# Queries and keys loaded in pieces of 64 partitions, and the stage behind v put in order by estimated engine times

## The chip, the cores and the metric

The kernel runs on one core of a Trainium2 chip. The metric is the device time of one execution in microseconds. TensorE (PE) multiplies, VectorE (DVE), ScalarE (ACT) and GpSimd (POOL) do the elementwise work, and SyncE (SP) issues nearly all transfers between DRAM and the on-chip memory; 16 DMA engines carry them.

## The reference

One encoder layer on `x` of 1024 tokens by 1024 channels, in float32. Eight heads (group A) use chunked softmax attention with a bias, eight heads (group B) stick-breaking attention; head width is 64.

```python
h = rmsnorm(x, norm1_g)
qa, ka, va, qb, kb, vb = split(h @ w_in)
# group A: each 64-frame chunk sees itself and the 8 chunks before it
p  = softmax(where(valid, qa @ ka.T * 64**-0.5 + bias, -1e30));  ya = p @ va
# group B: strictly causal, no softmax
z  = qb @ kb.T * 64**-0.5
log_beta = log_sigmoid(z)
log_1m   = where(causal, log_beta - z, 0)
suffix   = reverse_cumsum(log_1m) - log_1m
yb = where(causal, exp(log_beta + suffix), 0) @ vb
x = x + concat(rmsnorm(ya, norm_a_g), rmsnorm(yb, norm_b_g)) @ w_out
u = causal_depthwise_conv3(rmsnorm(x, norm2_g) @ w_ffn_in) + conv_b
x = x + (silu(gate(u)) * value(u)) @ w_ffn_out
return rmsnorm(x, final_g)
```

## The kernel before

**Precision.** A product of two float32 matrices is made of three matmuls: each operand is split into a high part (a copy rounded to `fp32r`, on ACT) and a low part (the difference, on DVE or POOL), and high x high, high x low and low x high are summed (`mm3`, `split`, `sub`). One step of such a product, 128 x 128 by 128 x 512, is three matmuls with 512 columns.

**The stages, in order.** (1) *v*: `all_v` makes the 1024 x 1024 values by a Strassen-like scheme with seven products for eight blocks, and writes them to DRAM (`v_d`, by `give`). (2) *Behind v*: `first_query` makes the query block 4, and four calls of `early` make the queries and keys of the pairs of heads 0 to 3, by the same scheme: seven calls of `product`, each 12 matmuls, into the accumulators `ea`, `eb`, `ec`, `ee`, with copies on ACT between them (`eb` starts from `ea`, `ec` from `eb`, `em` and `eu` take `ee` and `eb`). The left operands come from class `Pieces`: raw weights (`bring_raw`) are added to and subtracted from each other (`make`) and split. Two right operands, t1 and t2, were kept in DRAM during v and are brought back and split there (`bring_back`, `split_again`). Every finished query or key block is scaled, split, and written to DRAM as a high and a low part (`q_d`, `k_d`). (3) *Stage b*: stick-breaking, 4 pairs of heads with 8 query blocks of 128 each. For each block and head, `scores` makes z (lines 910 and 911), ACT takes the sigmoid (928), DVE a scan (919) and a difference (923), PE transposes (946), ACT copies (950), and PE multiplies with v (960). (4) *Stage a*: chunked attention, likewise (1010, 1011; 1027, 1041; 1062, 1066; 1075). (5) *Output projection* (`pa`, `pb`, line 147), then the feed-forward part (`u_*`, `dz`, ...).

**Loads of queries and keys.** For every pair of heads, `load_qk` (line 803 issues them) loads six tiles of 128 partitions x 1024: `qa` and `qb` hold the high part of a head's queries in one half of the partitions and the low part in the other; `ka`, `kb` hold the high part of the keys twice, and `la`, `lb` the low part twice. One matmul against `k` and one against `l` then give the whole product. Each tile is one transfer of 512 KB, whose source in DRAM has two groups of 64 rows:

```python
def twice(part, h):
    return k_d[n][part][None, h, :].to_broadcast([2, 64, T])
moves = [
    [(q, q_d[n][:, h, :]), (k, twice(0, h)), (l, twice(1, h))]
    for h, q, k, l in ((A, qa, ka, la), (B, qb, kb, lb))
]
```

**What sets the order.** The order on each engine is written out by the program. From stage b on, a planner (class `Flow`) does it: PE's order is fixed by the code, which tells the planner how long each step takes (`flow.work`); all other work is put in as chains of operations, each with an engine and an estimated time (`on_v`, `on_s`, `on_g`, `load`), and the planner records the operation that can start first. `need` makes PE's place in the order wait for a chain. Between the steps of stages b and a, PE gets "filler": the projections of the pairs 4 to 7 (`project_qk`, 7 of 16 steps) and half of the output projection (`out_b`); `RATE_B`, `RATES_A` and the leads set how much per step. The stages v and behind v are before the planner: there the operations stand in the order in which the code calls them, on DVE, ACT, POOL and SP alike. SP works in order: a transfer that waits for its data, or for room in its queue, holds everything behind it.

Of the kernel before, what the change touches and what calls it, by code (L numbers as in the profile page):

```python
# [36 lines left out]
RATE_B, LEAD_B = 8.0, 4.0  # L37
# [25 lines left out]
def tile_hybrid_block(  # L63
# [128 lines left out]
    with tc.tile_pool(name="kp", bufs=2) as kp:  # L192
# [48 lines left out]
        def all_v():  # L241
# [128 lines left out]
            def split_again(t):  # L370
                S.copy(t[:, lo], r32(t[:, hi]))
                sub(t[:, hi], r32(t[:, hi]), t[:, lo])
# [29 lines left out]
            def extra(n):  # L402
# [23 lines left out]
                if steps[n] == (4, 0):  # L426
                    lead["h"], lead["l"] = [
                        wp.tile([P, D], F32R, tag=t, name=f"q4_{t}") for t in ("wh", "wl")
                    ]
                    S.copy(lead["h"], lead["r"])  # L430
                    for r in halves:
                        sub(lead["l"][:, r], lead["r"][:, r], lead["h"][:, r], GP)
                if steps[n] == (4, 1):
                    give(m5, 1, 1)
                    give(u2, 0, 1)
                if steps[n] == (4, 2):
                    for k in range(KT):
                        bring_back(k)
                    ahead.append(Pieces(0))
                    ahead[0].make("s1")  # L440
                    ahead[0].split("s1")
                if steps[n] == (4, 3):
                    give(staged("c21"), 1, 0, Y)
                    bring_raw(1, 0)
                    bring_raw(1, 1)
                    bring_raw(2, 2)
                    bring_raw(2, 3)
# [37 lines left out]
            again_all.append(lambda: [split_again(t) for t in again])  # L485
# [33 lines left out]
        raws, ahead, lead, again_all = {}, [], {}, []  # L519
# [11 lines left out]
        class Pieces:  # L531


            def __init__(self, n):
                self.n, (self.q, self.k) = n, raws.pop(n)
                q, k = self.q, self.k
                self.p, self.src = {}, {
                    "s1": k[:, lo], "s2": q[:, lo], "s3": q[:, lo], "s4": q[:, hi], "a22": k[:, hi]
                }

            def whole(self):
                wh, wl = [
                    wp.tile([P, D], F32R, tag=t, name=f"qk{self.n}{t}") for t in ("wh", "wl")
                ]
                split(wh, wl, self.q)
                self.p["a11"], self.p["a12"] = (wh[:, lo], wl[:, lo]), (wh[:, hi], wl[:, hi])

            def make(self, what):
                q, k = self.q, self.k
                if what == "s1":  # L550
                    plus(k[:, lo], k[:, lo], k[:, hi], V)
                elif what == "s2":
                    minus(q[:, lo], k[:, lo], q[:, lo], V)
                elif what == "s4":
                    minus(q[:, hi], q[:, hi], q[:, lo], V)
                else:
                    minus(q[:, lo], q[:, lo], k[:, hi], V)

            def split(self, what):
                tag = {"s1": "r0", "s2": "r2", "s3": "r1", "s4": "r3"}.get(what)  # L560
                if tag:
                    t = pools["sbuf"].tile([P, T], F32R, tag=tag, name=f"{what}_{self.n}", bufs=1)
                    h, l = t[:, lo], t[:, hi]
                else:
                    h = kp.tile([P, GW], F32R, tag="sq", name=f"{what}h_{self.n}", bufs=1)
                    l = pools["sbuf"].tile([P, GW], F32R, tag="c", name=f"{what}l_{self.n}", bufs=1)
                self.p[what] = h, l
                split(h, l, self.src[what])

        S.preload_act_table_set("sqrt_and_others")  # L570
        right = all_v()
# [72 lines left out]
        flow = Flow()  # L644


# [41 lines left out]
        class Banks:  # L688


            def __init__(self, make, wait):
                self.make, self.wait, self.users = make, wait, deque([[], []])
# [4 lines left out]
            def get(self, name):  # L697
# [3 lines left out]
                return self.make(name), mine  # L701

# [91 lines left out]
        def load_qk(n):  # L794
# [3 lines left out]
            ts = [slot(s + i, f"{x}{n}", F32R) for i, x in enumerate(names)]  # L798
            qk_of[n] = ts
            qa, qb, ka, kb, la, lb = ts  # L800

            def both(t, src):
                nc.sync.dma_start(r32(t), src)  # L803
# [8 lines left out]
            qk_chains[n] = [  # L812
                flow.add(*(load(512, lambda m=m: both(*m)) for m in ms), after=qk_kept[n]) for ms in moves
            ]

        def advance():

            n = len(qk_of)
            if n < 8 and at["qk"] >= n - 2 and (n < 4 or len(qk_kept[n]) == (8 if n > 4 else 4)):
                load_qk(n)  # L820
# [62 lines left out]
        class BlockB:  # L883
# [14 lines left out]
            def scores(self, h):  # L898
                i, nk = self.i, self.nk
                qa, qb, ka, kb, la, lb = qk_of[self.n]  # L900
# [81 lines left out]
        class BlockA:  # L982
# [8 lines left out]
            def scores(self, h):  # L991
                p, i, nk = self.p, self.i, self.nk
                qa, qb, ka, kb, la, lb = qk_of[self.n]
# [183 lines left out]
        def product(o, left, what, start=True):  # L1177
            wh, wl = left
            for k, (th, tl) in enumerate(right[what]):
                for i, (w, t) in enumerate(((wh, th), (wh, tl), (wl, th))):  # L1180
# [4 lines left out]
            flow.work(2.72)  # L1185

        def early_out(n, what, src, r, f=None):

            if f is None:
                f = kp.tile([P, GW], F32, tag="tmp", name=f"e{what}{n}f", bufs=3)  # L1190
            V.scalar_tensor_tensor(
                out=f, in0=src, scalar=0.125 if what == "q" else 1.0, in1=rb1[:, r],
                op0=ALU.mult, op1=ALU.mult,
            )
            h = kp.tile([P, GW], F32R, tag="tmp", name=f"e{what}{n}h", bufs=3)
            S.copy(h, f)
            sub(f.bitcast(F32R), f, h)
            nc.sync.dma_start(kept_at(n, what, 0)[:, r], r32(h))
            nc.sync.dma_start(kept_at(n, what, 1)[:, r], f)

        def early(n):

            own = ahead[n]
            if n < 3:
                ahead.append(Pieces(n + 1))
            nxt = ahead[n + 1] if n < 3 else None
            a, e = zbank(f"ea{n}"), zbank(f"ee{n}")
            b, c = med(f"eb{n}"), pj(f"ec{n}")
            m5, u2 = [kp.tile([P, GW], F32, tag="eb", name=f"e{x}{n}") for x in ("m5", "u2")]
            if not nxt:  # L1210
                fetch()
            product(a, own.p["a11"], "b11")
            S.copy(b, a)
# [1133 lines left out]
```

## Time and profile before

| | us |
|---|---|
| median of 3 runs (1584.89 to 1586.72) | 1585.81 |
| profiled execution, its own time | 1587.85 |
| its span, first to last instruction | 1586.0 |
| TensorE busy in the span | 1222.8 |
| first matmul of stage b / of stage a / of feed-forward | 206.7 / 567.2 / 930.4 |

Columns of the views: a row of the windows has the stretch in us, its length, the busy us (and instructions) of PE, PE's weight load, DVE, ACT and POOL, then the granted TensorE clock as a share, the mean busy share of the 16 DMA engines, and GB/s. A row of SP's order in time has the start, the time for which the issue occupied SP, and the transfer. A row of a group has its count, then busy us and mean ns of one, then the idle time before them and what ended it. A row of waits has the waiting engine and line, what it waited for, total us, times, longest. A row of the chain has start, length and what it was. SPq is SP's queue, L a line of the program. A matmul's own duration in a group overlaps the next one's; lengths of runs in the chain do not.

### The profile page before, as it was taken

How to read it: one execution, taken by the hardware profiler on the slowest of the kernel's cores; microseconds unless marked ns; L12 is line 12 of the kernel's file. 1: busy time of each engine (PE TensorE's matmuls, PEld its weight loads, DVE VectorE, ACT ScalarE, POOL GpSimd, SP SyncE). 2: the span in 40 equal slices, each digit the busy share in tenths (PEclk: the TensorE clock that was granted, in tenths of full speed). 3: DMA queues.
4: the chain of work that ended last, by engine and by line, in shares of the span. 5: the costliest groups of instructions: out<-in, count | busy, mean ns of one | idle time of the engine just before them, and what ended most of it. 6: DMA issues, size and time to landing. Idle time of an engine off the chain costs nothing.

```text
span 1586.0 us, 17350 instructions
## 1 busy us (share of the span) xinstructions
PE 1222.8 (77%) x6428; PEld 1013.1 (64%) x6428; DVE 948.0 (60%) x1451; ACT 693.9 (44%) x1234; POOL 152.4 (10%) x156
## 2 busy tenths in 40 slices
PE   9989716443535380917559999999999999999997
PEld 7778515333434260815548788888888888888887
DVE  7857305324333340705437499877777777897996
ACT  7754203222324140705337346555555555544434
POOL 0000201000000010101101420000000000123215
PEclk9999957776768695967869999999999999999998
DMA  7463222213131312225221231222222222933003
GB/s 270 155 249 140 108 97 98 75 53 101 63 101 64 100 75 97 84 92 172 73 81 41 90 136 67 93 82 91 81 88 85 81 80 94 399 111 140 1 1 107
DMA packets 72211, 166.94 MB, mean 105 GB/s; under 512 B 6199, under 2 KB 21687, under 8 KB 72126
## 3 DMA queue, kind: packets, MB, share of 16 engines
q1 hardware_dynamic: 71982, 165.72, 29.7%
q8 instruction: 51, 0.84, 0.2%
q14 instruction: 34, 0.28, 0.1%
q10 hardware_dynamic: 144, 0.11, 0.0%
HBM read 118.60 MB, written 47.20 MB: 105 GB/s over the span
## 4 chain that ended last, share of the span: by engine, by line
PE 58%; SPq 19%; DMA 14%; DVE 5%; ACT 2%; issue 1%; POOL 0%; DVEq 0%; ACTq 0%; POOLq 0%
SPq L803 12%; PE u_a L1762 7%; PE u_c L1762 7%; PE u_e L1762 7%; PE dz L2261 6%; DMA lb<-k_d 4%; PE u_b L1762 3%; PE dj L2261 3%; PE dm L2261 3%; PE v_x L493 3%; PE pa L147 2%; DMA spill<-yb 2%; DMA la<-k_d 2%; PE v_y L493 2%; DMA bias<-in_toep_dram 2%; DMA q_d<-q_f 2%
## 5 line engine op out<-in xcount | busy, mean ns | idle before, releaser
L910 PE MATMUL zb<-kb,qb 128*128 128x512 f32 (+3 forms) x48 | 20.1, 419 | 144.1 <-DVE acts L919 144.1
L919 DVE TENSOR_TENSOR_SCAN acts<-zb,first 128x128 f32<-128x128 f32 (+7 forms) x64 | 86.4, 1351 | 64.6 <-ACT zb L928 64.5
L928 ACT ACTIVATE zb<-zb 128x128 f32<-128x128 f32 (+7 forms) x64 | 41.0, 641 | 174.1 <-PE zb L911 173.9
L1062 PE MATMUL tpa<-ident,pa 128*128 128x128 f32 x240 | 42.0, 298 | 96.1 <-DVE rn L1099 46.4
L910 PEld LDWEIGHTS zb<-kb,qb 128*128 128x128 f32 x48 | 10.3, 215 | 146.9 <-DVE acts L919 146.0
L1062 PEld LDWEIGHTS tpa<-ident,pa 128*128 128x128 f32 x240 | 30.1, 151 | 104.9 <-ACT pa L1034 48.4
L1351 DVE SCALAR_TENSOR_TENSOR yb<-y,cst,yb 128x512 fp32r<-128x512 f32 x8 | 6.0, 750 | 141.2 <-DMA spill<-yb 136.5
L1041 ACT ACTIVATE pa<-sa,sta 128x640 f32<-128x640 f32 (+4 forms) x64 | 42.5, 665 | 81.0 <-DVE sta L1044 48.0
L1786 DVE SCALAR_TENSOR_TENSOR vt<-cv,cst,vt 128x1023 f32<-128x1023 f32 (+1 forms) x44 | 58.2, 1322 | 3.7 <-ACT vt L1780 2.9
L1786 DVE SCALAR_TENSOR_TENSOR gt<-cg,cst,gt 128x1023 f32<-128x1023 f32 (+1 forms) x44 | 56.4, 1281 | 0.8
L1066 ACT COPY pta<-tpa 128x512 f32<-128x512 f32 (+3 forms) x80 | 36.3, 478 | 39.8 <-PE tpa L1062 39.7
L950 ACT COPY tb<-tpb 128x128 f32<-128x128 f32 (+3 forms) x96 | 43.2, 484 | 9.7 <-PE tpb L946 8.9
L946 PE MATMUL tpb<-ident,acts 128*128 128x128 f32 x288 | 47.1, 294 | 0.0
L911 PE MATMUL zb<-la,qa 128*128 128x512 f32 (+3 forms) x48 | 17.0, 360 | 38.5 <-DMA la<-k_d 38.5
L1780 ACT ACTIVATE gt<-cg,cst 128x1024 f32<-128x1024 f32 x22 | 27.4, 1245 | 36.4 <-DVE cg L1654 36.4
L1027 DVE TENSOR_REDUCE sta<-sa 128x1 f32<-128x640 f32 (+4 forms) x64 | 41.9, 655 | 1.4
L1651 DVE TENSOR_TENSOR up_r<-up_r 128x512 f32<-128x512 f32 x60 | 41.2, 687 | 0.8
L946 PEld LDWEIGHTS tpb<-ident,acts 128*128 128x128 f32 x288 | 36.2, 150 | 8.3 <-issue 2.8
L125 POOL TENSOR_TENSOR dx_0wl<-dr,dx_0wh 128x512 fp32r<-128x512 f32 x1 | 1.4, 1370 | 412.3 <-ACT dx_0wh L2028 412.3
L765 DVE SCALAR_TENSOR_TENSOR k_f<-k_p,rb 128x512 f32<-128x512 f32 x8 | 5.5, 687 | 53.9 <-DMA q_d<-q_f 48.5
L911 PEld LDWEIGHTS zb<-la,qa 128*128 128x128 f32 x48 | 9.6, 199 | 40.4 <-DMA la<-k_d 39.0
L910 PE MATMUL zb<-ka,qa 128*128 128x512 f32 (+3 forms) x48 | 18.1, 379 | 20.3 <-DMA ka<-k_d 20.3
(1417 smaller groups left out, 4160.4 us busy)
## 6 DMA issues: line engine op xcount, KB each, us to landing
up_r<-in_w_up_dram SPq DMA_DIRECT2D x44, 512.0 KB
act<-vt SPq DMA_DIRECT2D x22, 512.0 KB
dr<-in_w_dn_dram SPq DMA_DIRECT2D x20, 512.0 KB
dr<-act SPq DMA_DIRECT2D x20, 512.0 KB
wv<-in_w_v_dram SPq DMA_DIRECT2D x16, 256.0 KB
xin<-in_xT_dram SPq DMA_DIRECT2D x16, 256.0 KB
row<-in_x_rows_dram SPq DMA_DIRECT2D x16, 256.0 KB
raw<-in_w_in_dram SPq DMA_DIRECT2D x8, 512.0 KB
```

Of the source, the lines that this page charges most:

```text
L493: PE.matmul(bank[j], t[:, cols(j)], w, start=p in (1, 5) and k == 0 and i == 0, stop=k == 3 and i == 2, skip_group_check=True,)
L803: nc.sync.dma_start(r32(t), src)
L910: PE.matmul(z[:, o : o + n], q[:, cols(i)], k[:, ks], start=True, stop=False)
L919: V.tensor_tensor_scan(out=a[:, :w], data0=z, data1=first[:, :w], initial=1.0, op0=ALU.mult, op1=ALU.max,)
L946: PE.transpose(tp[:, cols(b)], self.a[h][:, cols(b0 + b)], ident)
L950: mine.append(flow.add(on_s(m * P, lambda o=o, tp=tp: S.copy(o, tp))))
L1027: V.tensor_reduce(out=st[:, 0:1], in_=full, axis=AX.XY if nk == 5 else AX.X, op=ALU.max, negate=True,)
L1041: on_s(w + 170, lambda: S.activation(po, full, AF.Exp, bias=st[:, 0:1], accum_out=st[:, 1:2])),
L1062: PE.transpose(tp[:, cols(b)], self.pr[src][:, cols(c)], ident)
L1762: PE.matmul(o, w[:, cols(k)], t, start=start and k == 0 and i == 0, stop=k == 3 and i == 2, skip_group_check=True,)
L1786: V.scalar_tensor_tensor(out=t[:, : T - lag], in0=o[:, lag:], scalar=c1(c + ct), in1=t[:, : T - lag], op0=ALU.mult, op1=ALU.add,)
L2261: PE.matmul(o[m], w[:, cols(m)], t, start=i in (0, 1, 4, 5) and p == ps_[0] and j == 0, stop=p == ps_[-1] and j == 2, skip_group_check=True,)
```

## The change

- `load_qk` issues, instead of six transfers of 128 partitions, twelve of 64 partitions x 1024 (256 KB each): for every tile its two halves apart. For pair 0, the pieces of `q` and the high part of `k` are asked for during the third call of `early`, the low part of `k` during the fourth.
- The stage behind v goes through the planner: the additions, splits, copies, outputs and raw loads of `Pieces`, `split_again`, `first_query` and `early` are chains with estimated times. The copies that PE waits for (`copy_chain`) have a due time two units in front of the others. `early_out` is replaced by `spill_qk` (with the high part of keys on POOL) and `out_in_place`. Two of the eight low parts of t1 and t2 go to POOL.
- At the end of v, `bring_back` is called two steps earlier, the first pieces are made and split before the second half of v is given out, and the raw loads for pair 2 are left out there and asked for in `early`.
- `RATE_B` is 10 instead of 8.

```diff
-RATE_B, LEAD_B = 8.0, 4.0
+BACK, BACK_STEP = 1.0, 0.6
+BEHIND_V = {"V": 1.0, "S": 5.0, "D": 7.0}
+RATE_B, LEAD_B = 10.0, 4.0
...
                 if steps[n] == (4, 1):
-                    give(m5, 1, 1)
+                    ahead.append(Pieces(0))
+                    ahead[0].whole(flow)
                     give(u2, 0, 1)
                 if steps[n] == (4, 2):
-                    for k in range(KT):
-                        bring_back(k)
-                    ahead.append(Pieces(0))
-                    ahead[0].make("s1")
-                    ahead[0].split("s1")
+                    for what in ("s1", "s2"):
+                        ahead[0].make(what, flow)
+                        ahead[0].split(what, flow)
+                    flow.drain()
+                    give(m5, 1, 1)
                 if steps[n] == (4, 3):
                     give(staged("c21"), 1, 0, Y)
                     bring_raw(1, 0)
                     bring_raw(1, 1)
-                    bring_raw(2, 2)
-                    bring_raw(2, 3)
...
-            def both(t, src):
-                nc.sync.dma_start(r32(t), src)
-
-            def twice(part, h):
-                return k_d[n][part][None, h, :].to_broadcast([2, 64, T])
-
-            moves = [
-                [(q, q_d[n][:, h, :]), (k, twice(0, h)), (l, twice(1, h))]
-                for h, q, k, l in ((A, qa, ka, la), (B, qb, kb, lb))
-            ]
-            qk_chains[n] = [
-                flow.add(*(load(512, lambda m=m: both(*m)) for m in ms), after=qk_kept[n]) for ms in moves
-            ]
+            def bring(i, x, d, y):
+                if x == A if i % 2 == 0 else x == B:
+                    qk_of.setdefault(n, {})[i] = slot(s + i, f"{names[i]}{n}", F32R)
+                nc.sync.dma_start(r32(qk_of[n][i][x, :]), d[y, :])
+
+            def moves(h):
+                x, y = (A, B) if h == 0 else (B, A)
+                tensors = (((h, q_d[n][0], q_d[n][1]), (2 + h, k_d[n][0], k_d[n][0])), ((4 + h, k_d[n][1], k_d[n][1]),))
+                return [
+                    move for p in ((0, 1) if part is None else (part,)) for i, d0, d1 in tensors[p]
+                    for move in ((i, x, d0, x), (i, y, d1, x))
+                ]
+
+            qk_chains.setdefault(n, []).extend(
+                flow.add(*(load(256, lambda m=m: bring(*m)) for m in moves(h)), after=[*qk_kept[n], *after])
+                for h in range(2)
+            )
...
+        def copy_chain(do, after=()):
+            c = flow.add(on_s(GW, do), after=after)
+            c.due = -2.0
+            return c
...
-            product(a, own.p["a11"], "b11")
-            S.copy(b, a)
-            own.split("a22")
-            if n == 1:
-                bring_raw(3, 11)
-                bring_raw(3, 10)
-            if nxt:
-                nxt.whole()
-                nxt.make("s1")
-                nxt.make("s2")
-            product(e, own.p["s1"], "t1")
-            S.copy(m5, e)
+            product(a, own, "a11", "b11")
+            b, mb = bs.get(f"eb{n}")
+            cb = copy_chain(lambda: S.copy(b, a))
+            own.split("a22", flow)
+            if nxt:
+                nxt.whole(flow)
+                nxt.make("s1", flow)
+                nxt.make("s2", flow)
+                nxt.make("s4", flow)
+            else:
+                fetch()
+            if n in (0, 1):
+                flow.emit(own.ready["a22"])
+                load_raw(n + 2, ((2, 3), (11, 10))[n], [own.ready["a22"]])
+            e, me = zs.get(f"ee{n}")
+            product(e, own, "s1", "t1")
+            cm = copy_chain(lambda: to(m5, "m5", e), after=[eb_last[0]])
...
-                    own.whole()
-                    own.make("s2")
-                    own.split("s2")
-                    again_all[0]()
-                    early_out(4, "q", outs[0], lo)
...
+            flow.free.update(BEHIND_V)
+            lead["again"]()
+            for what in ("s4", "s3"):
+                own.make(what, flow)
+                own.split(what, flow)
...
+                mine.append(spill_qk(4, "q", {g: o}, g))
```

How the rows move, in the two places of which the prediction speaks. First, SP, around the loads for pair 1 at the start of stage b (`q_d`, `k_d` are the queries and keys in DRAM; each row is one transfer, with the size of its target). Before:

```order
L803 DMA qa_1639<-q_d_138 128x1x1024
L803 DMA qb_1640<-q_d_138 128x1x1024
L783 DMA k_d_149<-k_h_1669 128x512
L783 DMA k_d_149<-k_f_1661 128x512
L803 DMA ka_1641<-k_d_146 128x1x1024
L803 DMA kb_1642<-k_d_146 128x1x1024
L803 DMA la_1643<-k_d_146 128x1x1024
L803 DMA lb_1644<-k_d_146 128x1x1024
```

And with the change:

```order
L849 DMA qa_1710<-q_d_138 64x1024
L849 DMA qb_1719<-q_d_138 64x1024
L830 DMA k_d_148<-k_f_1614 128x512
L1256 DMA q_d_140<-eu_1500 128x512
L849 DMA qa_1710<-q_d_138 64x1024
L849 DMA qb_1719<-q_d_138 64x1024
L849 DMA ka_1786<-k_d_146 64x1024
L849 DMA kb_1790<-k_d_146 64x1024
L849 DMA ka_1786<-k_d_146 64x1024
L849 DMA kb_1790<-k_d_146 64x1024
L849 DMA la_1831<-k_d_146 64x1024
L849 DMA lb_1850<-k_d_146 64x1024
```

Every tile is now filled by two rows of 64 partitions, and the outputs of pair 3 (`k_d_148`, `q_d_140`) stand between them. Second, ACT from the splits of t1 and t2 to the first copy into `eb`, which PE's third product waits for (`s_0` are high parts of the left operands, `eq4h` and `q_h` high parts of query block 4, which is written to DRAM from there). Before:

```order
L371 CAST t_6_833<-t_6_833 128x512
L371 CAST t_7_835<-t_7_835 128x512
L1196 CAST eq4h<-eq4f 128x512
L128 CAST s_0_970<-raw_11_683 128x512
L128 CAST s_0_974<-raw_11_683 128x512
L1196 CAST eq4h<-eq4f 128x512
L1213 COPY eb_986<-ea_984 128x512
```

And with the change:

```order
L735 CAST s_0_950<-raw_11_683 128x512
L378 CAST t_6_789<-t_6_789 128x512
L378 CAST t_7_791<-t_7_791 128x512
L735 CAST s_0_962<-raw_11_683 128x512
L827 CAST q_h_969<-q_f_921 128x512
L1286 COPY eb_986<-ea_964 128x512
```

One of the two casts for query block 4 now stands behind the copy.

More of the change, by code (lines that the diff above doesn't have):

```diff
@@ L483, in begin @@
                     parts(6, 0)
-            again_all.append(lambda: [split_again(t) for t in again])
+            lead["again"] = lambda: [split_again(k) for k in range(KT)]
             begin(-1)
@@ L529, in bring_raw, with load_raw @@
             mine.append(t)
[L531 to L543, printed above, removed]
-                ]
[L545 to L571, printed above, removed]
+        def load_raw(n, tags, after):
+            raw_chains[n] = [
+                flow.add(load(512, lambda x=x: bring_raw(n, x)), after=after) for x in tags
+            ]
         class Chain:
@@ L1184, in product @@
                     )
[L1185 to L1193, printed above, removed]
-            )
[L1195 to L1199, printed above, removed]
+                flow.work(0.68)
@@ new lines, in out_in_place, with scale, high, keep @@
+        def out_in_place(n, what, t, r, after):
+            x = {}
+            def scale():
+                V.scalar_tensor_tensor(
+                    out=t["f"], in0=t["f"], scalar=0.125 if what == "q" else 1.0, in1=rb1[:, r],
+                    op0=ALU.mult, op1=ALU.mult,
+                )
+            def high():
+                x["h"] = kp.tile([P, GW], F32R, tag="tmp", name=f"e{what}{n}h", bufs=3)
+                S.copy(x["h"], t["f"])
+            def keep(part, src):
+                return load(256, lambda: nc.sync.dma_start((q_d if what == "q" else k_d)[n][part][:, r], r32(src())))
+            _, low = fs.chain(
+                on_s(GW, high), on_v(GW, lambda: sub(t["f"].bitcast(F32R), t["f"], x["h"]), "VL"),
+                keep(0, lambda: x["h"]), keep(1, lambda: t["f"]), after=[flow.add(on_v(GW, scale), after=after)],
+            )
+            qk_kept[n].append(low)
+            return low
@@ L1323, in need @@
             advance()
-            while n not in qk_of:
+            while n not in qk_chains:
                 c = next(fill)
```

195 lines of the change are left out of this document (137 added, 58 removed).

## Prediction

> **What bounds the kernel now.** I read the page first, then the busy time by stage, then the waits, then SP's own queue in order of time.
>
> ```profile
> span 1586.0 us, 17350 instructions
> ...
> PE   9989716443535380917559999999999999999997
> ...
> PEclk9999957776768695967869999999999999999998
> ...
> PE 58%; SPq 19%; DMA 14%; DVE 5%; ACT 2%; issue 1%; POOL 0%; DVEq 0%; ACTq 0%; POOLq 0%
> ```
>
> Slices 5 to 23 (about 200 to 910 us) show TensorE half idle at a low granted clock, and 33% of the chain of waits is SP's queue and transfers. The same by stage (v; the stage behind v; its end; stick-breaking b; chunked a; output projection; feed-forward):
>
> ```profile
> core 0: us, PE busy (x) PEld busy (x) DVE busy (x) ACT busy (x) POOL busy (x), PEclk, DMA share, GB/s
> 0.00:85.00 85.00, 82.98 (x347) 64.64 (x348) 64.73 (x104) 65.18 (x128) 3.33 (x10) 1.00 0.63 218
> 85.00:177.00 92.00, 86.98 (x371) 70.43 (x370) 56.90 (x84) 41.98 (x72) 3.71 (x5) 0.96 0.48 173
> 177.00:206.75 29.75, 9.45 (x43) 7.44 (x41) 5.25 (x7) 1.24 (x2) 4.73 (x7) 0.74 0.24 96
> 206.75:567.00 360.25, 166.22 (x1241) 138.90 (x1242) 124.50 (x157) 101.27 (x201) 16.81 (x21) 0.72 0.24 84
> 567.00:862.50 295.50, 166.41 (x1182) 140.70 (x1181) 124.66 (x315) 115.90 (x256) 28.78 (x39) 0.77 0.27 91
> 862.50:930.40 67.90, 64.82 (x336) 52.92 (x335) 41.36 (x71) 26.21 (x46) 24.50 (x23) 1.00 0.28 94
> 930.40:1586.00 655.60, 645.95 (x2918) 538.09 (x2916) 530.58 (x716) 342.08 (x533) 70.51 (x53) 0.99 0.28 101
> ```
>
> From 177 to 862.5 us, 685.5 us pass and PE is busy for 342 (9.45 + 166.22 + 166.41); DVE has 254 and ACT 218, so no engine fills it. Before 177 and after 862.5 PE is nearly full. What is late between is on SP:
>
> ```profile
> 309.22 11.71 SPq L803 DMA_DIRECT2D ka<-k_d  x1
> ...
> 340.62 9.78 SPq L803 DMA_DIRECT2D lb<-k_d  x1
> 395.43 0.54 SPq L803 DMA_DIRECT2D qa<-q_d  x1
> ...
> 90.00:100.00 10.00, 10.00 (x46) 8.24 (x45) 8.15 (x13) 5.77 (x11) 0.00 (x0) 1.00 1.02 358
> 340.00:350.00 10.00, 0.00 (x0) 0.00 (x0) 0.00 (x0) 0.00 (x0) 0.00 (x0) 0.50 0.13 52
> ```
>
> An issue with a free queue takes 0.54 us; with a full one it blocks until an earlier transfer has drained, 9.78 us for 512 KB. In the row 340 to 350 nothing runs but these loads: 0.13 of 16 DMA engines is 2 engines, at 52 GB/s, where 90 to 100 us shows all 16 at 358. 512 KB at 52 GB/s is 10 us, which is the blocked time. So the 48 loads (8 pairs of heads, six each) need 48 x 9.78 = 469 us of two DMA engines, and everything behind them on SP waits too (the v loads, yb's spills, the bias):
>
> ```profile
> PE zb L910 <- DVE acts L919: 144.1, 5, 46.6
> DVE yb L1351 <- DMA spill<-yb: 136.5, 4, 48.1
> PE zb L911 <- DMA la<-k_d: 38.5, 2, 21.8
> PE tpa L1062 <- DVE rn L1099: 46.4, 1, 46.4
> ```
>
> The waits on acts and rn name an engine that had long been done; the length of 46 us is that of four to five blocked issues.
>
> **The pieces.** The change replaces six loads of 512 KB whose outermost dimension on the DRAM side is 2 by twelve of 256 KB, 64 rows of 4 KB each. The bytes stay at 25.2 MB. No row of this trace has a 64-partition load. Bounds for one piece: 256 KB at the 358 GB/s of the row 90 to 100, 0.73 us, or still two engines at 52 GB/s, 4.9 us. Even at a quarter of the engines (105 GB/s, twice the row 340 to 350) it would be 2.4 us, or 29 us per pair of heads, under the 37 to 40 us which such a pair gets below. I take 0.73, since every plain load with rows of this size is in the fast regime: 96 pieces, 70 us, beside TensorE's work. The 48 extra issues cost SP 0.54 us each, 26 us, while SP has nothing else to do; if that cover were gone, +26.
>
> The Trainium skill, "DMA: Bandwidth & Descriptors", Rules for kernel authors, says that an outermost dimension smaller than 16 confines a DMA to at most that many engines. The row 340 to 350 agrees (2 of 16); by that rule a piece of 64 rows gets all 16, and the sum stays as it is.
>
> **What is left when the loads are early.** TensorE's work from 177 to 862.5 at full clock, by counts and by durations in rows at clock 1.00:
>
> ```profile
> 115.76 2.77 PE ec L1181 x12
> L911 PE MATMUL zb<-lb,qb x48: 278/388/796, 240.4 to 553.3; 128*128 128x512 f32 x20, 128*128 128x256 f32 x12, 128*128 128x384 f32 x8, 128*128 128x320 f32 x8
> L1011 PE MATMUL sa<-lb,qb x48: 278/308/637, 568.0 to 865.6; 128*128 128x320 f32 x32, 128*128 128x256 f32 x8, 128*128 128x512 f32 x4, 128*128 128x384 f32 x4
> L946 PE MATMUL tpb<-ident,acts 128*128 128x128 f32 x288 | 47.1, 294 | 0.0
> L1062 PE MATMUL tpa<-ident,pa 128*128 128x128 f32 x240 | 42.0, 298 | 96.1 <-DVE rn L1099 46.4 <-ACT pa L1034 46.0 <-DVE yq L1450 2.2
> 246.34 0.87 PE tpb L946 x8
> L960 PE MATMUL yb<-tb,dv 128*64 128x128 f32 x448 | 30.9, 283 | 0.0
> L960 PE MATMUL yb<-tb,v 128*64 128x128 f32 x128 | 13.5, 303 | 0.0
> L1075 PE MATMUL yy<-pta,v 128*64 128x128 f32 x480 | 29.7, 276 | 0.0
> 742.25 1.68 PE yy L1075 x28
> L147 PE MATMUL pb<-yh,wo_h 128*128 128x512 f32 x64 | 28.5, 446 | 0.0
> ```
>
> A 512-column matmul takes 2.77/12 = 0.231 us, 0.451 ns a column. Scores of b: 20 x 512 + 12 x 256 + 8 x 384 + 8 x 320 = 18944 columns, four such groups (ka, kb, la, lb), 34.2 us. Scores of a: 15872 columns x 4, 28.6. Transposes: 528 x 0.87/8, 57.4. Outputs: 480 records in a and 576 (448 + 128) in b, x 1.68/28, 63.4. Filler: 7 projections of 48 matmuls (16 steps of three) and 144 of the 192 pb (three rows like the one quoted; 48 stand behind 862.5), 480 x 0.231, 110.9. Row sums and spreads, some 60 short ones: 8. Together 302.5 us; the 342 measured held the slow clock after each stop.
>
> How much of the time is PE busy? Two rows from stretches that were not blocked:
>
> ```profile
> 760.00:770.00 10.00, 10.00 (x84) 8.43 (x83) 8.74 (x20) 6.30 (x13) 2.80 (x4) 1.00 0.13 53
> 840.00:850.00 10.00, 9.87 (x92) 8.54 (x91) 7.69 (x20) 6.46 (x14) 1.58 (x3) 1.00 0.46 158
> ```
>
> 0.99; but these follow stops in which DVE and ACT caught up. I take 0.93: 302.5/0.93 = 325 us, with DVE at 254/325 = 78% and ACT at 67%. The bounds are 302.5 (no gap) and 378 (0.80).
>
> **The stage behind v.** From 85 to 177 PE loses its time at one place:
>
> ```profile
> 100.00:110.00 10.00, 4.98 (x17) 3.71 (x16) 6.17 (x9) 4.31 (x7) 0.00 (x0) 0.80 0.70 276
> 110.00:120.00 10.00, 10.00 (x39) 7.99 (x38) 6.11 (x10) 2.83 (x5) 0.00 (x0) 0.86 0.16 56
> PEld eb L1181 <- ACT eb L1213: 5.8, 2, 5.5
> 99.87 6.38 DMA q_d<-eq4h
> 120.00:130.00 10.00, 10.00 (x45) 8.18 (x44) 6.56 (x10) 4.95 (x9) 0.00 (x0) 1.00 0.39 144
> ```
>
> 17 and 39 matmuls where the next window has 45: 34 are missing, 34 x 0.231 = 7.9 us. TensorE waits for ACT's copy into eb, which stands behind a cast that waits for a transfer of q. The change puts the eb copy ahead of the second of these casts and keeps two raw loads (1 MB) out of the queue there. That can win back at most 7.9; where a new wait appears in the same place it wins nothing, and a raw load of 1 MB that is now asked for later takes 2.9 us at 358 GB/s, so -3 at worst. I take 6: DVE and ACT have slack there (56.90 and 41.98 of 92). The changed end of v reorders ACT work of 65 us in 85; costed at nothing, its cover is PE's four steps of lead there. b's rate of filler goes from 8 to 10: 36 more projection matmuls stand in b and as many fewer in a, 8.3 us moved, none added.
>
> **Sum.** The stage behind v ends at 177 - 6 = 171; b and a take 325, to 496; the output projection keeps its 67.9, to 564, where feed-forward began at 930.4. 930.4 - 564 = 366 less than the profiled execution's 1587.85 (span 1586.0 and 1.85 around it): 1222. That execution lies 2.0 over the median of 1585.81, so **1220 us**.
>
> **Rivals.**
> *Other waits take the place* (b and a at 0.80 instead of 0.93): 378 instead of 325, +53, 1273. For it: DVE's order in b is scan after scan, 64 of them, and in a the row 760 to 770 has DVE at 0.87. Against: no undisturbed row shows PE under 0.95 there.
> *Splitting gives nothing:* two halves share the queue as one did, 4.9 us each, 469 us in all. Then only the 6 us of the early stage are won: 1587.85 - 6 - 2 = 1580. Against it stand the 2 engines of the row 340 to 350, which a wide load need not have. The Trainium skill says, same page and section, of two transfers to disjoint partition halves "Don't bother": they share the same engines, one 128-partition transfer is better. The trace bears it out only for loads that already have 16 engines, which these lack.
> *Slower:* a piece costs the queue as much as a load did, 9.78 us whatever its size (one DMA engine for 64 rows at half of 52 GB/s gives that too). SP's load line would need 96 x 9.78 = 939 us, 470 more, on the path that already is the chain: 2050. It decides from 4.9 us a piece on. Against it: the blocked time equals bytes over rate, not a fixed cost.
>
> **How the numbers follow.** Forecast 0.81, other waits 0.12, nothing won 0.04, slower 0.03. A measurement of this kernel tells about 0.2% (3 us) from no change. Faster: 0.81 + 0.12 and half of the third, 0.95; same 0.02; slower 0.03. The forecast's own range: 302.5 us for b and a and 8 early, 1196, to 0.86 (352 us, +27) and nothing early, 1253. The range takes in the first rival with 26 us of issues uncovered: 1192 to 1299.
>
> **What would show it.** In the changed profile the load line's issues should take about half a microsecond, a stretch with only these loads should show far over 0.13 of the DMA engines, the chain should be PE for over 85% of the span, slices at clock 5 should be gone, and the first feed-forward matmul should stand near 564 us. PE short of 45 matmuls in the 10 us around the first eb product would show the 6 us wrong. SP issues of 4 us and more would show the pieces wrong; PE idle on scans of DVE or on ACT in a, the 0.93.

## The result and the profile after

| | before | after |
|---|---|---|
| median (runs) | 1586.16 us (4, 1584.89 to 1586.72) | 1220.49 us (4, 1219.31 to 1221.48) |
| ratio, 95% interval | | 0.7695 (0.7682 to 0.7709) |
| profiled execution, span | 1587.85, 1586.0 | 1221.42, 1219.7 |
| first feed-forward matmul | 930.21 | 565.05 |

The forecast was 1220 us with a range of 1192 to 1299. (The 930.4 us from which it counts is the start of the second feed-forward matmul before the change; the first starts at 930.21.) The page of the changed kernel, its lines on the span, on TensorE and its clock by slices, and on the chain of waits:

```profile
span 1219.7 us, 17426 instructions
...
PE   9999999999999989899999999999999999999997
...
PEclk9999999999999999999999999999999999999998
...
PE 84%; DVE 6%; DMA 4%; ACT 3%; SPq 1%; issue 1%; POOL 0%; DVEq 0%; ACTq 0%; POOLq 0%
```

The half-empty slices and the low clock are gone. SP's queue and the transfers fell from 33% of the chain to 5%, and TensorE is 84% of it. By stage (v; the stage behind v; lead into b; b; a; output projection; feed-forward; the columns are those of the windows before):

```profile
0.00:85.00 85.00, 82.48 (x346) 64.21 (x347) 66.14 (x106) 64.26 (x125) 3.33 (x10) 1.00 0.62 214
85.00:174.50 89.50, 89.50 (x394) 73.14 (x394) 56.97 (x85) 43.09 (x73) 10.92 (x12) 1.00 0.71 229
174.50:200.00 25.50, 24.89 (x160) 21.02 (x159) 20.71 (x26) 13.57 (x25) 6.91 (x11) 1.00 0.97 265
200.00:334.00 134.00, 134.00 (x1138) 114.80 (x1137) 107.74 (x138) 88.09 (x176) 17.60 (x21) 1.00 0.65 178
334.00:499.00 165.00, 155.55 (x1200) 132.74 (x1198) 125.99 (x324) 116.98 (x261) 24.86 (x34) 0.98 0.55 153
499.00:565.00 66.00, 60.47 (x280) 49.34 (x280) 36.85 (x57) 24.03 (x40) 24.17 (x23) 0.95 0.29 96
565.00:1219.70 654.70, 645.93 (x2919) 538.01 (x2918) 530.32 (x717) 342.25 (x533) 70.81 (x53) 0.99 0.28 101
```

Nearly everything was gained between 85 and 565 us. TensorE has no gap at all in the stage behind v and in most of b; what is left lies in a (9.45 us without a matmul) and in the output projection (5.5). The load line of the changed kernel, one of its six tiles and the time from issue to landing (the three numbers are ns min/median/max, then the first and last start in us):

```profile
L849 SPq DMA_DIRECT2D kb<-k_d x16: 444/594/2816, 144.9 to 421.2; - x16
...
DMA to landing us min/median/max: 3.6/6.2/10.6
```

The issue of a piece took 0.51 to 0.60 us at the median, by tile; before, the loads of `ka`, `kb`, `la` and `lb` took 6.1 to 9.8 us at the median, those of `qa` and `qb` 0.51 to 0.54. With a median that short, most pieces find room in the queue at once; the longest of this tile is 2.8 us.

### The profile page after: what moved, and what is told of

It is laid out like the page before. It is cut to its first block, busy times and chain, and to the rows that moved or that the text cites. A ratio compares the mean times of both kernels' runs of the same rounds, so it can differ in the third digit from the quotient of the medians.

```text
span 1219.7 us, 17426 instructions
## 1 busy us (share of the span) xinstructions
PE 1192.8 (98%) x6428; PEld 993.2 (81%) x6428; DVE 944.7 (77%) x1449; ACT 692.3 (57%) x1230; POOL 158.6 (13%) x162
## 4 chain that ended last, share of the span: by engine, by line
PE 84%; DVE 6%; DMA 4%; ACT 3%; SPq 1%; issue 1%; POOL 0%; DVEq 0%; ACTq 0%; POOLq 0%
PE u_a L1845 9%; PE u_c L1845 9%; PE u_e L1845 8%; PE dz L2344 8%; PE u_b L1845 4%; PE dj L2344 4%; PE dm L2344 4%; PE v_x L503 3%; PE pa L151 3%; PE v_y L503 3%; PE yb L1008 3%; PE tpb L994 3%; PE q_p L151 2%; PE k_p L151 2%; PE yy L1123 2%; PE ee L1235 2%
## 5 line engine op out<-in xcount | busy, mean ns | idle before, releaser
L1110 PE MATMUL tpa<-ident,pa 128*128 128x128 f32 x240 | 39.3, 284 | 5.4 <-ACT pta L1114 2.2
L994 PE MATMUL tpb<-ident,acts 128*128 128x128 f32 x288 | 43.3, 277 | 0.0
L994 PEld LDWEIGHTS tpb<-ident,acts 128*128 128x128 f32 x288 | 33.1, 140 | 6.3 <-issue 2.6
L2032 ACT COPY u_b<-u_a 128x512 f32<-128x512 f32 x19 | 10.8, 571 | 38.1 <-PE u_a L1845 38.1
L1072 DVE TENSOR_TENSOR sa<-sa,bias 128x256 f32<-128x256 f32 (+1 forms) x64 | 26.3, 413 | 6.6 <-PE sa L1059 5.3
L1123 PE MATMUL yy<-pta,v 128*64 128x128 f32 x480 | 31.3, 285 | 0.0
L1123 PEld LDWEIGHTS yy<-pta,v 128*64 128x64 f32 x480 | 27.4, 143 | 3.4 <-issue 1.6
L1008 PE MATMUL yb<-tb,dv 128*64 128x128 f32 x448 | 29.2, 273 | 0.0
L1658 POOL TENSOR_TENSOR n_acc<-n_acc,n_sq 128x384 f32<-128x384 f32 (+2 forms) x23 | 24.1, 1047 | 28.9 <-ACT n_sq L1657 28.2
L129 POOL TENSOR_TENSOR wo_l<-wo_r,wo_h 128x256 fp32r<-128x256 f32 x28 | 20.1, 749 | 59.3 <-ACT wo_h L786 59.3
```

The costliest lines, as they stand in the source:

```text
L994: PE.transpose(tp[:, cols(b)], self.a[h][:, cols(b0 + b)], ident)
L1008: PE.matmul(yy[HS[h], :], (d if j else v)[:, off : off + 64], self.at[h][:, self.c0[h] + j * P : self.c0[h] + (j + 1) * P], start=j == 0, ...
L1110: PE.transpose(tp[:, cols(b)], self.pr[src][:, cols(c)], ident)
L1123: PE.matmul(yy[HS[h], :], v[:, (i + c) * P + h * 64 : (i + c) * P + (h + 1) * 64], self.pt[:, 4 * h + c if c < 4 else 8 + h, :], start=c = ...
```

## The experiments

Eleven kernels were run. Medians and ratios, each against the kernel before on the same chip:

| kernel | median, us | ratio | 95% |
|---|---|---|---|
| before, with the loads cut into halves and nothing else | 1224.95 | 0.7723 | 0.7711 to 0.7734 |
| the change, with 128-partition loads put back | 1552.62 | 0.9788 | 0.9769 to 0.9808 |
| the change, source rows in 2 groups | 1540.77 | 0.9713 | 0.9694 to 0.9733 |
| the change, source rows in 4 groups | 1322.34 | 0.8330 | 0.8315 to 0.8346 |
| the change, source rows in 8 groups | 1251.27 | 0.7884 | 0.7873 to 0.7895 |
| the change, every piece as two of 32 partitions | 1219.84 | 0.7688 | 0.7678 to 0.7699 |
| the change, `RATE_B` 8 | 1212.15 | 0.7639 | 0.7629 to 0.7650 |
| the change, `RATE_B` 7 | 1212.60 | 0.7647 | 0.7637 to 0.7658 |
| the change, `RATE_B` 6 | 1210.47 | 0.7632 | 0.7622 to 0.7643 |
| the change, no due time for the copies | 1220.49 | 0.7695 | 0.7684 to 0.7705 |
| halved loads only, with a cast moved behind the first `eb` copy | 1223.84 | 0.7716 | 0.7704 to 0.7727 |

### Halved loads alone

```diff
             def both(t, src):
-                nc.sync.dma_start(r32(t), src)
+                nc.sync.dma_start(r32(t[A, :]), src[0])
+                nc.sync.dma_start(r32(t[B, :]), src[1])
```

> The kernel before, with each of the 48 loads of queries and keys issued as two of 64 partitions and nothing else changed. Theory (the loads on two DMA engines are the stall; the new order behind v is worth its 8 us and no more): 1220 + 8 for the gap at the first eb copy, so 1225 to 1240. Rival (the planned order is what keeps TensorE fed once the loads are fast): above 1300.

1224.95 us, just under the lower end of what was expected: 1586.16 - 1224.95 = 361.2 of the 365.7 us come from this one edit. TensorE's waits between 85 and 215 us in this kernel (us in total, times, longest):

```profile
PE eb L1182 <- ACT eb L1214: 5.5, 1, 5.5
PE zb L912 <- DMA la<-k_d: 3.9, 1, 3.9
```

The wait for `eb` stands as it did before the change, and the first scores of b wait for a late load. Both are gone in the changed kernel, so 9.4 us should part the two kernels, yet only 4.5 do. Something in the change costs time again; the runs on `RATE_B` below name it.

### The order alone

```diff
-                for move in ((i, x, d0, x), (i, y, d1, x))
...
-                nc.sync.dma_start(r32(qk_of[n][i][x, :]), d[y, :])
+                nc.sync.dma_start(r32(qk_of[n][i]), src)
```

with `src` as it was before the change, the source of 128 partitions in two groups of 64 rows; all else is as in the changed kernel.

> The changed kernel, with its loads put back to one transfer of 128 partitions from two groups of 64 rows; order behind v and rate as changed. Theory: the stall is back, 1570 to 1590, with the stage behind v still ending near 174 us. Rival (order counts): under 1450.

1552.62 us, 17 below the lower end: without fast loads the order is worth 33.5 us, not the 16 at most that were expected. The ratio's interval, 0.9769 to 0.9808, leaves open whether this is 2%, but both runs (1552.19 and 1553.05) are far under every run of the kernel before. The stage behind v did not end early. This kernel's SP in order of time, and its longest wait of TensorE between 85 and 215 us, with the wait of ACT in front of it:

```profile
137.20 0.60 SPq L848 DMA_DIRECT2D qa<-q_d  x1
...
138.50 7.44 SPq L830 DMA_DIRECT2D k_d<-k_h  x1
...
148.68 9.15 SPq L848 DMA_DIRECT2D kb<-k_d  x1
157.93 9.60 SPq L830 DMA_DIRECT2D k_d<-k_f  x1
```

```profile
PE eb L1234 <- ACT eb L1285: 22.5, 1, 22.5
ACT ek2h L1252 <- DMA k_d<-k_f: 20.0, 1, 20.0
```

Outputs of keys, which have nothing to do with these loads, are held for 7 to 10 us behind them. ACT's cast for the next key block waits 20.0 us for such an output, ACT's copy into `eb` stands behind that cast, and TensorE loses 22.5 us there, so the stage ended near 199 us. But the loads for pair 0 are asked for at 137.20, where the kernel before asks at 171.50:

```profile
171.50 0.61 SPq L803 DMA_DIRECT2D qa<-q_d  x1
```

That is 34.3 us earlier, and feed-forward starts at 895.6 instead of 930.2, 34.6 earlier. So the end seems to move with the start of the slow queue and not with the end of the stage in front of it. The expectation had left out that, where the queue is the bound, asking earlier can move the end by as much. It was not tested by itself. The next run, which asks at 137.1 too, agrees in direction and not in size: its feed-forward starts at 885.5, 44.7 us earlier.

### What makes a load slow: size, partitions or the outermost dimension

The halved loads differ from those before in three ways: half the bytes, 64 partitions instead of 128, and an outermost dimension of 64 rows in DRAM instead of 2 groups. Three kernels keep pieces, bytes and partitions of the change and alter only the third (and with it the order in which the rows are read): the 64 rows are read as 2, 4 or 8 interleaved groups. Queries and keys have their rows permuted in the same way by this, so their products stay what they were.

```diff
-                nc.sync.dma_start(r32(qk_of[n][i][x, :]), d[y, :])
+                nc.sync.dma_start(r32(qk_of[n][i][x, :]), d[y, :].rearrange("(b a) t -> a b t", a=2))
```

> The changed kernel with the same 96 pieces of 64 partitions and 4 KB rows, but the source read as 2 interleaved groups of 32 rows, so that its outermost dimension is 2 (queries and keys are permuted alike, so z is the same). Theory (the outermost dimension sets the number of DMA engines): 2 engines again, 4.9 us a piece, 1560 to 1600, DMA share 0.13 in a stretch with only these loads. Rival (half the partitions or half the bytes is what made them fast): 1220.

1540.77 us: nearly the whole gain is gone. Two of its load rows, and one window of it in which only the loads run:

```profile
L849 SPq DMA_DIRECT2D ka<-k_d x16: 492/4592/6691, 143.7 to 719.3; - x16
L849 SPq DMA_DIRECT2D kb<-k_d x16: 856/4791/6617, 152.9 to 726.0; - x16
```

```profile
250.00:260.00 10.00, 0.00 (x0) 0.00 (x0) 0.00 (x0) 0.00 (x0) 0.00 (x0) 0.62 0.13 53
```

For these two tiles the median issue is 4.6 to 4.8 us where 4.9 was worked out for 256 KB on two engines; the other four, `qa` and `qb` at 0.5 us and `la` and `lb` at 2.1 to 2.5, more often find room in the queue. The share of 0.13 at 53 GB/s is that of the kernel before. So neither the number of partitions nor the bytes made the loads slow; the outermost dimension of 2 did. The time misses the expected range by 19 us on the lower side; asking early, as in the run before, is a likely reason, but it is not shown.

With `a=4`:

> As the one with outermost dimension 2, with 4 groups of 16 rows. Theory: 4 engines, 105 GB/s, 2.4 us a piece, 29 us a pair of heads against 37 to 40 us of work, so nearly hidden: 1222 to 1260. If the queue's order makes the others wait too: up to 1350. Rival (partitions or bytes): 1220.

1322.34 us, 102 over the changed kernel, inside the range given for the case that the others wait too. Its SP in order of time, and two windows:

```profile
291.57 2.23 SPq L920 DMA_DIRECT2D dv<-v_d  x1
293.89 9.82 SPq L921 DMA_DIRECT2D v<-v_d  x1
303.81 4.60 SPq L1440 DMA_DIRECT2D spill<-yb  x1
```

```profile
300.00:310.00 10.00, 5.64 (x56) 4.55 (x54) 0.38 (x2) 1.17 (x3) 0.00 (x0) 0.96 0.51 148
310.00:320.00 10.00, 1.45 (x4) 0.94 (x5) 5.30 (x6) 2.21 (x5) 0.00 (x0) 0.50 0.37 142
```

Here L849 loads are on the way in front, and it is the next transfers that pay: the issue of v blocks for 9.82 us, the spill of yb behind it for 4.60, and from 300 us on DVE, ACT and then TensorE run dry. The DMA engines as a whole have much room there (their share is 0.4 to 0.5), yet what comes next in SP's order waits behind the narrow transfers. Over 85 to 600 us of this trace TensorE's largest wait is 35.7 us, in eight parts, for DVE's scans; not all of the 102 us were assigned.

With `a=8`:

> As the kernels with outermost dimension 2 and 4, with 8 groups of 8 rows. If the number of engines equals the outermost dimension: 8 engines, 210 GB/s, 1.2 us a piece, 15 us a pair. From 2, 4 (1541, 1322) and 64 rows (1220) the stall that is left should be small: 1222 to 1245. If only the full 16 engines hide the loads: above 1260.

1251.27 us, 31 over the changed kernel, between the ranges that the two theories gave. Its SP in order of time, then DVE in order of time (the bracket is the idle time before an instruction and what ended it):

```profile
262.23 6.11 SPq L921 DMA_DIRECT2D v<-v_d  x1
268.43 5.63 SPq L1440 DMA_DIRECT2D spill<-yb  x1
```

```profile
277.47 1.23 DVE L925 TENSOR_TENSOR dv<-v,dv 128x1024 f32<-128x1024 f32 x1 [5.46 <-DMA v<-v_d]
...
279.28 1.75 DVE L967 TENSOR_TENSOR_SCAN acts<-zb,first 128x768 f32<-128x768 f32 x1
```

Every load still issues in under 0.6 us at the median, so the load line alone looks healthy. The cost shows one transfer later: v blocks for 6.11 us, DVE's difference on v waits 5.46 us for it, and the scan behind it on DVE, on which TensorE depends, starts late. This is one instance; the 31 us were not assigned one by one.

How many engines the pieces get can be read from windows in which almost only they are moved, with 4 groups, with 8, and in the changed kernel:

```profile
527.00:535.00 8.00, 0.69 (x14) 0.45 (x10) 0.00 (x0) 0.00 (x0) 0.00 (x0) 0.75 0.26 105
```

```profile
456.00:461.00 5.00, 4.32 (x51) 3.65 (x49) 0.00 (x0) 0.75 (x3) 0.00 (x0) 1.00 0.51 129
```

```profile
424.00:429.00 5.00, 5.00 (x37) 4.21 (x37) 4.89 (x13) 4.30 (x9) 0.11 (x1) 1.00 1.04 222
```

The shares of 0.26, 0.51 and 1.04 are 4, 8 and all 16 engines (the share adds up the times of packets, so it can come out a little over 1). The rate does not follow the engines: 105 GB/s with 4 is what was worked out, but 8 engines move 129 GB/s and not 210. A piece then takes 2.0 us and a pair of heads 24, where the expectation had 1.2 and 15. Why 8 engines move so little more than 4 is not shown.

The four kernels in a row give 1540.77, 1322.34, 1251.27 and 1220.49 us for an outermost dimension of 2, 4, 8 and 64. This fits the rule of the Trainium skill ("DMA: Bandwidth & Descriptors", Rules for kernel authors) that an outermost dimension under 16 confines a transfer to at most that many DMA engines. The same section's advice not to bother with halves on disjoint partitions does not hold for such a source: halving alone gave a ratio of 0.7723. The next run halves again, pieces that already have 16 engines, and there nothing is won, as the advice says.

### Still smaller pieces

```diff
-                nc.sync.dma_start(r32(qk_of[n][i][x, :]), d[y, :])
+                for o in (0, 32):
+                    xx, yy_ = slice(x.start + o, x.start + o + 32), slice(y.start + o, y.start + o + 32)
+                    nc.sync.dma_start(r32(qk_of[n][i][xx, :]), d[yy_, :])
```

> The changed kernel with each piece of 64 partitions issued as two of 32 (192 transfers of 128 KB): 96 more issues on SP, about 50 us of its time. Theory (SP is idle there and the issues are hidden): 1219 to 1224. Rival (a transfer costs the queue a fixed time, so more of them cost more): 1240 and up.

1219.84 us, no difference. Its load row for the same tile:

```profile
L851 SPq DMA_DIRECT2D kb<-k_d x32: 302/419/2957, 144.5 to 424.6; - x32
```

96 more issues of 0.42 us are hidden beside TensorE's work, and a transfer has no fixed price that could be felt here.

### The rate of filler in stage b

```diff
-RATE_B, LEAD_B = 10.0, 4.0
+RATE_B, LEAD_B = 8.0, 4.0
```

> The changed kernel with the filler rate of stage b back at 8: 36 projection matmuls (8.3 us) move from b to a. PE was 100% busy in b with 10, and in a ran out of filler from 440 to 460 us and at 510 us (about 10 us idle, at a lower clock behind it). Theory (the filler is missing in a): 1211 to 1218. Rival (b becomes bound by DVE, 108 of 134 us busy, and idles by what is moved): 1220 to 1228.

1212.15 us: with the rate of the kernel before, the changed kernel is 8.3 us faster. The 10 us windows of stage a show where, first with rate 10, then with rate 8:

```profile
440.00:450.00 10.00, 6.78 (x55) 5.24 (x56) 6.81 (x17) 6.67 (x16) 0.88 (x2) 0.83 0.16 55
450.00:460.00 10.00, 7.84 (x64) 6.41 (x60) 6.04 (x19) 6.46 (x18) 1.26 (x1) 0.83 0.16 52
```

```profile
440.00:450.00 10.00, 9.74 (x96) 8.40 (x93) 7.98 (x25) 7.85 (x21) 1.29 (x1) 1.00 0.36 93
450.00:460.00 10.00, 10.00 (x64) 8.48 (x63) 8.89 (x22) 6.65 (x17) 0.00 (x0) 1.00 0.18 56
```

At rate 10 more of the projections stand in b, where TensorE is full, and the last one is done at 385 us, against 405 at rate 8. From 440 to 460 us no filler at all then stands between the transposes and the scores, where rate 8 has 36 matmuls of the output projection. TensorE waits there, mostly for ACT, and the mean granted clock of each window is 0.83. At rate 8 these two windows are nearly full.

The same line with 7, then with 6:

> The changed kernel with a filler rate of 7 in stage b. With 10 stage a lacked filler (1220.5), with 8 b was 98% and a 98% busy (1212.2). Theory (near the balance): 1210 to 1215. Rival (b now idles more than a gains): above 1216.

> As with 7, with a rate of 6. Theory (DVE, 130 of 157 us busy in b at a rate of 8, becomes the bound of b, and PE idles there): 1214 to 1222. Rival (filler late is as good as filler early): 1209 to 1213.

1212.60 and 1210.47 us. For 7 the expectation held. For 6 it took a turn upward, as b would now run short; there is none, the rival was right. By the intervals of their ratios the three rates do not part, though every run of 6 (at most 1210.87) lies under every run of 7 (at least 1212.41). The stages from 174.5 to 565 us (b with its lead; a; output projection), at rate 8 and then at rate 6:

```profile
174.50:334.00 159.50, 156.94 (x1277) 131.38 (x1276) 129.68 (x165) 100.76 (x202) 23.46 (x30) 1.00 0.70 187
334.00:499.00 165.00, 162.25 (x1255) 138.24 (x1255) 128.90 (x330) 119.80 (x270) 27.43 (x40) 1.00 0.55 158
499.00:565.00 66.00, 63.16 (x299) 51.82 (x298) 41.93 (x63) 25.41 (x40) 23.83 (x21) 1.00 0.41 136
```

```profile
174.50:334.00 159.50, 155.48 (x1269) 129.96 (x1268) 131.61 (x168) 101.67 (x203) 22.22 (x27) 1.00 0.69 188
334.00:499.00 165.00, 162.96 (x1260) 139.20 (x1259) 125.67 (x325) 119.66 (x269) 29.04 (x42) 1.00 0.55 157
499.00:565.00 66.00, 64.67 (x307) 53.43 (x306) 44.20 (x66) 25.96 (x40) 23.16 (x21) 1.00 0.40 136
```

In these 390.5 us TensorE is busy for 382.4 and 383.1 us, against 374.9 at rate 10 (24.89 + 134.00 + 155.55 + 60.47): more work has been done by the same moment, 7.4 and 8.2 us of it, most of the time that is won. Rate 6 has the lowest median of all kernels run, 10 us under the changed kernel.

### The due time of the copies

```diff
-            c.due = -2.0
+            c.due = 0.0
```

> The changed kernel with the due time of the copies that TensorE waits for set to 0, as for other work, instead of two units ahead; this puts three splits in front of the copies of rb and one in front of a copy of em. Theory (the gap went with the planned order of the loads and of the outputs of query block 4, not with the due time): 1219 to 1222. Rival (the copies in front are what closes the gap): 1225 to 1229.

1220.49 us, the same as with it. The copies that TensorE waits for are in time without being put in front; the order in which the chains are handed to the planner is enough.

### A cast moved, with the loads halved

This is the kernel with halved loads only, with one step moved: the second output of query block 4 (its cast on ACT waits for a transfer) is asked for behind the first copy into `eb`:

```diff
-                    early_out(4, "q", outs[1], hi)
+                    lead["o"] = outs[1]
...
             S.copy(b, a)
+            if not n:
+                early_out(4, "q", lead["o"], hi)
             own.split("a22")
```

> The kernel before with the loads in pieces, and the second output of query block 4 issued behind the first copy into eb instead of in front of it. Theory (PE's gap of 5.5 us there and the slow clock behind it came from that cast, which waited for a transfer): 7 to 8 us under the kernel with the loads alone (1225), so 1216 to 1220. Rival (the copy of t1 and t2 or another buffer is late next): 1222 to 1225.

1223.84 us (1221.54 to 1226.3) against 1224.95 without the move: the time lies in the rival's range and not in the theory's, and the intervals overlap, so by the time the move is worth nothing that can be told. The traces do differ. TensorE's waits between 85 and 215 us with the cast moved, then the window 100 to 110 us without and with the move:

```profile
PE eb L1182 <- ACT eb L1214: 2.0, 2, 1.9
PE ec L1182 <- ACT ec L1230: 0.8, 1, 0.8
```

```profile
100.00:110.00 10.00, 4.55 (x16) 3.32 (x15) 5.74 (x9) 4.31 (x7) 0.00 (x0) 0.86 0.71 277
```

```profile
100.00:110.00 10.00, 8.04 (x34) 5.88 (x32) 7.02 (x11) 4.72 (x8) 0.00 (x0) 1.00 0.61 238
```

16 matmuls become 34 in this window, and the wait for `eb` shrinks from 5.5 to 2.0 us. In the trace the cast of query block 4 was thus most of what held the copy, but not all: two casts of raw pieces still stand in front of it on ACT. That these are the rest was not tried.

## Why the prediction was right

**The loads.** This step held, but for the rate of a piece. The rows that it named as signs are there: issues of about half a microsecond, a chain with 84% TensorE (over 85% was asked, so one point short), no slices at clock 5, feed-forward at 565.05 where 564 was forecast. The rival *splitting gives nothing* is refuted by the halved loads alone, and *slower*, the fixed price per transfer, by the 32-partition pieces. The claim that two engines were the cause, and neither the bytes nor the partitions of a load, is borne out by the three groupings. The 0.73 us a piece was too short: it took the 358 GB/s of a window that moved other transfers, while the pieces run at 222 GB/s on all 16 engines, 1.18 us each (a piece lands 6.2 us after its issue at the median, but several are on the way at a time). This cost nothing, as 96 x 1.18 = 113 us still lie beside TensorE's work. The 48 extra issues, costed at nothing, cost nothing either: even 96 more do not show.

**"Even at a quarter of the engines" was wrong.** The text took 29 us per pair of heads at four engines to be hidden under the 37 to 40 us that a pair gets. The kernel with 4 groups is that case, and it is 102 us slower; even half of the engines cost 31. The 105 GB/s and 2.4 us a piece held. The sum of transfer times compared with the time available left out the order on SP: the v loads and the spills wait behind the narrow transfers, and each is needed at a time of its own.

**The stage behind v: right gain, wrong end.** The text let this stage end at 177 before and at 171 after. The trace of before has its last product after that:

```profile
181.98 0.39 PE L1181 MATMUL ec<-th,a22l 128*128 128x512 f32 x1
182.21 0.39 PE L147 MATMUL k_p<-hTh,k_h 128*128 128x512 f32 x1
```

and after the change:

```profile
174.16 0.39 PE L1235 MATMUL ec<-th,a22l 128*128 128x512 f32 x1
174.38 0.39 PE L151 MATMUL k_p<-hTh,k_h 128*128 128x512 f32 x1
```

The gain is 182.2 - 174.4 = 7.8 us, where 6 was taken out of a bound of 7.9. The two windows that had lacked 34 matmuls, and the one behind them, are full in the changed kernel, where 45 was the mark:

```profile
100.00:110.00 10.00, 10.00 (x45) 8.13 (x44) 9.96 (x17) 5.32 (x9) 0.00 (x0) 1.00 0.89 282
110.00:120.00 10.00, 10.00 (x45) 8.16 (x44) 8.50 (x13) 3.82 (x7) 1.03 (x1) 1.00 0.63 221
120.00:130.00 10.00, 10.00 (x45) 8.15 (x44) 6.40 (x9) 4.56 (x8) 0.00 (x0) 1.00 0.45 155
```

The end of 177 came from the place at which the chain of waits leaves TensorE, 5.2 us before its last product. So 174.4 stands where 171 was forecast, 3.4 late.

**b and a: the sum right, its two factors not.** 325 us were forecast for both; from 174.4 to 499 it is 324.6. But the 302.5 us of work counted from groups are 314.4 busy us in the windows after, and the 0.93 of busy time is 0.97. The two errors of 4% cancel, which is luck. Counting each matmul of that trace from its start to the next one's start, or to its own end if that comes first, shows which terms were off: the scores take 73 us, not 62.8, and the filler 121 us (492 matmuls, not 480), not 110.9; the transposes take 52 us, not 57.4, the row sums and spreads 5, not 8; the outputs took the 63 that were counted. A clock below 1 in a (0.98 of 165 us) is 3 us of the total. Nor is the idle time spread as one share: none in b, nearly all in a. The rival of 0.80 is refuted by the 0.97.

**"b's rate of filler goes from 8 to 10: 8.3 us moved, none added" was wrong.** Moving it costs 8.3 us, as the run with rate 8 shows: at rate 10, b and its lead have 0.6 us without a matmul and a has 9.5; at rate 8 it is 2.6 and 2.8. The filler left a stage whose gaps it filled for one that had almost none. (That 8.3 us of matmuls were moved and 8.3 us were lost is a coincidence.) The prediction priced the matmuls, which are the same, and not the gaps that they had covered. With this, the whole difference splits into three steps, each between two kernels that were run: halved loads -361.2 us, all else of the change at rate 8 -12.8 (1224.95 to 1212.15), the rate +8.3. The 5.5 and 3.9 us of waits that go away are 9.4 of the 12.8; the other 3.4 were not assigned.

**The end.** The output projection took 66.0 us where 67.9 was taken over from before, and feed-forward 654.7 where 655.6. Together 2.8 us less, which offsets most of the 3.4 above. So the mechanism of the loads was right, and that the total was met within 1 us is luck: terms that were off by 3 to 12 us happened to cancel. The range's lower end of 1192 is 4 us under the 1196 that was worked out, and no term stands for these 4.

## What to carry to other kernels

Read the number of DMA engines from a window in which only one kind of transfer runs; where it is far below 16, look at the outermost dimension of the source and cut the transfer so that each piece has many rows, even at twice the transfers. A narrow transfer is dear through what stands behind it in the issuing queue, so compare due times in that queue and not only bytes with a stage's length. Filler matmuls are worth what they cover: before moving them, look which stage has gaps.

## What was not expected of the hardware

- Half of the 16 DMA engines (8 groups) is not enough here, although the DMA share of the changed kernel is only 0.55 to 0.65 in b and a: +31 us, with issues of 4 to 6 us among the transfers behind.
- With these rows of 4 KB an engine moved 26 GB/s where 2 or 4 were in use (52/2, 105/4), 16 where 8 were (129/8) and 14 where all 16 were (222/16). The order in which the rows are read differs between these kernels too, and the cause is open.
- A transfer's issue by SP in the kernels with fast loads took 0.42 us for 128 KB and 0.51 to 0.60 us for 256 KB at the median; doubling the number of these issues, from 96 to 192 in some 290 us, cost nothing that can be measured.
- A blocked queue reaches work that does not use the slow loads at all: with the order alone, stores of finished keys were held for 7.44 and 9.60 us, and TensorE lost 22.5 us at one copy in the same stretch.
